# Plain and seven-product quads in turn, wider low parts and an eighth seven-product quad in eleven chunk pairs of a hybrid decoder layer

## The chip, the core and the metric

The kernel runs on one core of one Trainium2 chip. The time is that of one execution on the device in microseconds (us); the median of three runs is given, and one more execution was taken by the hardware profiler. Engines are named TensorE (PE in the profile, PEld its weight loads), VectorE (DVE), ScalarE (ACT), GpSimd (POOL) and SyncE (SP, which issues the loads here).

## What is computed

One layer works on 256 tokens of width 4096, in float32. One projection of 4096 x 16384 makes the inputs of an attention group (q, k, v and a gate z, 16 heads of 128) and of a short convolution group (h, B, C and a gate z). Both are gated, put side by side and mapped by an output projection of 4096 x 4096; a residual and an RMSNorm follow. With 256 tokens the block-sparse attention is causal attention in one block, with a bias by distance. Cut to what matters:

```
u = rmsnorm(x, norm_gain)
q, k, v, z_a, hc, b, c, z_c = split(u @ w_in)            # 4096 x 16384
attn = causal_attention(q, k, v, rel_bias) * silu(z_a)
conv = b * short_conv(c * hc, conv_w) * silu(z_c)        # three taps
h = x + concat(attn, conv) @ w_out                       # 4096 x 4096
out = rmsnorm(h, final_gain)
```

## The kernel before

**Products.** The weights stream once from HBM and are the moving operand; the tokens are the stationary one. The 32 column chunks of 512 of the input projection are taken in 16 pairs (0 to 15, `PAIRS`), those of the output projection in four more (16 to 19). Each pair runs over 16 quads. A quad is a block product of 2 x 2 blocks: two token blocks of 128 by two blocks of 128 of the inner dimension, times those two inner blocks by two chunks of 512. A plain quad makes the eight block products. A quad in `SEVENS` makes seven, by Strassen's scheme in Winograd's form, from sums of weight blocks (made on VectorE) and sums of token blocks (made once). A plain quad feeds the accumulators 3, 8, 2 and 4; a seven-product quad feeds 1, 3, 2 and then 5, 7, 6, 4. Accumulator n is PSUM bank `p`n, and there are eight banks.

**One block product is three matmuls.** Each operand is split into a high part in the fast float32 format and a low part, the rest. `block` (L552 to L563) makes stationary high by high, stationary low by high and stationary high by low, each with 512 columns, on lines 561, 562 and 563. The weights are split as they come, in `split` (L475): ScalarE writes the high part (L506), VectorE subtracts it for the low part (L507). A unit is what is split and multiplied at once: a plain quad has two units of 1024 (four blocks each), a seven-product quad one of 1536 from the raw weights (three blocks) and two of 1024 from the sums (two each). High and low parts lie in rings of three slots (`RING`), and the split runs two units ahead of the products. The sums come from three VectorE additions (L488 to L490) into one buffer, raw weights from loads of 1 MB, two quads ahead (`load`, L443).

**Ends of a pair.** In every pair but 0, 1 and 16 the quads 0, 2, ... 12 have seven products and the odd ones and 14 eight, in the order 0 to 15. So after position 12 the accumulators 1, 5, 6 and 7 are complete. `early` (L333) reads them at once, in one ScalarE copy and four VectorE additions (L336 to L340), and their banks serve as scratch for side tasks during the last 24 blocks. `scaled` (L349) multiplies the four early values by the row scale on ScalarE. The other four accumulators are read at the pair's end (`two_done`, L354; for the output `out_end`, L422).

**Side tasks.** `tasks_of` gives a list: after so many blocks behind the last seven-product quad, run a task. In the odd pairs 1 to 7 these are `turn` (transposes of q and k, copied by ScalarE), `scores` (two matmuls, bias and maxima on VectorE, exponentials on ScalarE) and `probs` (transposes, copied by ScalarE) for four heads; in the pairs 2, 4, 6 and 8 `values` and `mixed`; in 10, 12, 14 and at the head of 16 `conv`. The token sums that a seven-product quad needs are made for some quads only in pair 1 and pair 16 (`RAISE`, `made_up`), and the output's token operands during pairs 15 and 16 (`M_AT`, `m_parts`).

A scheduling layer sets each engine's order from this program; it can differ from the listing's order where the layer found another instruction ready first.

## Time and profile before

| | |
|---|---|
| median of three runs | 1729.7 us (1729.67 to 1729.95) |
| the profiled execution | 1729.5 us |
| its span, first to last instruction | 1727.7 us |
| busy: TensorE, VectorE, ScalarE | 99%, 87%, 59% of the span |
| mean granted TensorE clock | 0.998 |
| moved by DMA | 370 MB, 214 GB/s over the span |

The profiled execution's own time is 1.8 us over its span. The busy share of an engine counts the time in which any of its instructions is recorded; on TensorE the records of successive matmuls overlap, so the share doesn't tell how fast they follow each other. The granted clock is 1.00 but at the very end: the higher of the two levels, 2.4 GHz.

### The profile page before, as it was taken

The numbers are of one execution on the slowest core, as the hardware profiler recorded it, in microseconds if no ns is written. First come the engines' busy times: TensorE is split into PE (matmuls) and PEld (weight loads), VectorE is DVE, ScalarE is ACT, GpSimd is POOL, SyncE is SP. The second block draws the span as 40 slices with busy tenths as digits, with TensorE's granted clock in tenths as the row PEclk, the third lists the DMA queues.
The fourth block names the chain that finished last, engine by engine and source line by source line (L and its number), as shares of the span: only waits on it lengthen the run. The fifth ranks groups of instructions, "written<-read, shape, count | busy, mean of one in ns | idle before, by whom it ended". The sixth has DMA issues, their size and how long they took to land.

```text
span 1727.7 us, 20841 instructions
## 1 busy us (share of the span) xinstructions
PE 1711.7 (99%) x7672; PEld 1406.9 (81%) x7672; DVE 1498.8 (87%) x1658; ACT 1026.1 (59%) x1135; POOL 0.7 (0%) x6
## 2 busy tenths in 40 slices
...
GB/s 321 299 248 211 188 202 207 203 183 210 202 203 187 213 193 214 182 196 218 198 212 203 204 217 198 198 206 220 196 218 208 265 277 266 207 212 207 195 215 175
DMA packets 66562, 370.29 MB, mean 214 GB/s; under 512 B 8955, under 2 KB 13852, under 8 KB 25756
## 3 DMA queue, kind: packets, MB, share of 16 engines
...
HBM read 359.76 MB, written 9.18 MB: 214 GB/s over the span
## 4 chain that ended last, share of the span: by engine, by line
PE 97%; DVE 1%; ACT 1%; issue 0%; DVEq 0%; ACTq 0%
PE p L563 32%; PE p L561 31%; PE p L562 31%; PE p L239 0%; PE p L246 0%; ACT hi L506 0%; DVE lo L507 0%; PE p L108 0%; PE p L263 0%; PE p L272 0%; PE p L274 0%; PE p L273 0%; PE p L247 0%; PE p L298 0%; PE p L320 0%
## 5 line engine op out<-in xcount | busy, mean ns | idle before, releaser
L561 PE MATMUL p<-hi,k 128*128 128x512 f32 x2406 | 944.8, 393 | 2.9 <-ACT hi L506 2.8
L562 PE MATMUL p<-hi,k 128*128 128x512 f32 x2406 | 937.0, 389 | 0.0
L563 PE MATMUL p<-lo,k 128*128 128x512 f32 x2406 | 928.9, 390 | 0.1
L507 DVE TENSOR_TENSOR lo<-raw,hi 128x1024 fp32r<-128x1024 f32 (+2 forms) x508 | 676.2, 1348 | 61.3 <-ACT hi L506 60.3
L506 ACT CAST hi<-raw 128x1024 fp32r<-128x1024 f32 (+2 forms) x508 | 583.0, 1156 | 244.1 <-PE p L562 202.3
L561 PEld LDWEIGHTS p<-hi,k 128*128 128x128 f32 x2406 | 451.9, 188 | 100.1 <-ACT hi L506 9.0
L563 PEld LDWEIGHTS p<-lo,k 128*128 128x128 f32 x2406 | 451.3, 188 | 99.2 <-DVE lo L507 3.8
L562 PEld LDWEIGHTS p<-hi,k 128*128 128x128 f32 x2406 | 452.0, 188 | 91.0 <-issue 0.6
L506 ACT CAST hi<-sum 128x1024 fp32r<-128x1024 f32 x260 | 273.9, 1054 | 402.1 <-PE p L562 251.8
L507 DVE TENSOR_TENSOR lo<-sum,hi 128x1024 fp32r<-128x1024 f32 x260 | 317.6, 1221 | 127.1 <-ACT hi L506 125.7
L488 DVE TENSOR_TENSOR sum<-raw 128x1024 f32<-128x1024 f32 x130 | 158.8, 1222 | 9.7 <-DMA raw<-in_w_dram 8.0
L490 DVE TENSOR_TENSOR sum<-sum,raw 128x512 f32<-128x512 f32 x130 | 89.1, 685 | 0.3
L489 DVE TENSOR_TENSOR sum<-sum,raw 128x512 f32<-128x512 f32 x130 | 89.1, 685 | 0.1
L349 ACT ACTIVATE e<-e,rT 128x512 f32<-128x512 f32 x56 | 38.2, 717 | 0.0
L127 ACT CAST k<-c 128x512 fp32r<-128x512 f32 (+3 forms) x35 | 19.6, 576 | 10.9 <-PE p L563 6.0
L128 DVE TENSOR_TENSOR k<-c,k 128x512 fp32r<-128x512 f32 (+3 forms) x35 | 21.7, 632 | 0.8 <-ACT k L127 0.8
L424 ACT ACTIVATE e<-hg 128x512 f32<-128x512 f32 x16 | 10.0, 627 | 11.3 <-DVE hg L422 11.0
L277 DVE SCALAR_TENSOR_TENSOR am<-p,st,z 128x128 f32<-128x128 f32 x32 | 9.7, 344 | 7.5 <-PE p L274 7.5
L124 DVE TENSOR_TENSOR c<-c 128x128 f32<-128x128 f32 x56 | 14.0, 285 | 2.0 <-ACT c L138 1.2
L324 DVE SCALAR_TENSOR_TENSOR y<-p,cw,y 128x255 f32<-128x255 f32 (+1 forms) x32 | 15.3, 477 | 0.3 <-ACT y L322 0.2
L153 DVE SCALAR_TENSOR_TENSOR k<-xr,g_sb,k 128x256 fp32r<-128x256 f32 x26 | 11.6, 479 | 4.5 <-ACT k L152 4.5
L254 ACT ACTIVATE lg<-lg,st 128x256 f32<-128x256 f32 (+1 forms) x32 | 14.3, 446 | 0.0
...
## 6 DMA issues: line engine op xcount, KB each, us to landing
raw<-in_w_dram SPq DMA_DIRECT2D x254, 1024.0 KB, 4.8
...
```

Of the source, the lines that this page charges most:

```text
L127: nc.scalar.copy(dst[:, :, 0], c)
L128: nc.vector.tensor_tensor(dst[:, :, 1], c, dst[:, :, 0].bitcast(F32), ALU.subtract)
L324: nc.vector.scalar_tensor_tensor(y[:, i:], ps[:, :S - i], cw[:, k, 2 - i:3 - i], y[:, i:], op0=ALU.mult, op1=ALU.add)
L349: nc.scalar.activation(e, e, AF.Copy, scale=r)
L488: nc.vector.tensor_tensor(t[:, :2], raw[:, 1:3], raw[:, :1].to_broadcast([P, 2, B]), ALU.add)
L489: nc.vector.tensor_tensor(t[:, 2], t[:, 0], raw[:, 2], ALU.add)
L490: nc.vector.tensor_tensor(t[:, 3], t[:, 2], raw[:, 3], ALU.add)
L506: nc.scalar.copy(hi[:, c], src[:, c])
L507: nc.vector.tensor_tensor(lo[:, c], src[:, c], hi[:, c].bitcast(F32), ALU.subtract)
L561: nc.tensor.matmul(acc[b_], a, h_, start=s0, stop=False)
L562: nc.tensor.matmul(acc[b_], b, h_, start=False, stop=False)
L563: nc.tensor.matmul(acc[b_], a, l_, start=False, stop=s1)
```

## The change

1. The order in a pair begins with a plain quad, and plain and seven-product quads take turns. A pattern per pair says which: `P` takes the next plain quad, `S` the next seven-product one.
2. In the pairs 2 to 8 (pattern `8`) and 9, 11, 13, 15 (pattern `n`) quad 14 has seven products as well. Its token operand holds eight blocks (`BOTH`), as other pairs use it plain, and its sums are made in pair 1.
3. In odd pairs the accumulators 1, 2, 3, ... lie on other banks (`SWAP`): 1 and 2, 3 and 5, 4 and 6, 7 and 8 change places.
4. A plain quad is one unit of 2048: two high parts of 1024, one low part of 2048. Slots of the rings hold 2048 (1536 before). Units of three blocks and more issue all matmuls on high parts ahead of those on low parts (`AHEAD_HI`).
5. Sums go to two buffers in turn in pairs 0 to 15.
6. The side tasks stand within 16 blocks (two plain quads) behind the last seven-product quad, the last two `probs` of a group at the head of the next pair (`heads_of`); in patterns `n` no task stands there but the scalings, which go into the last plain quad. The scratch that the loader of the program reserves is set to 1024.

```diff
+PATS = {"7": "PSPSPSPSPSPSPSPP", "8": "PSPSSPSPSSPSPSPP", "n": "PSPSPSPSSPSPSPSP", "e": "PSPSPSPSPSPSSPPP"}
+KIND = "01888888" "8n7n7n7n" "077e"
 RING = 3
+SLOT = 4
+LO = 4
+HI = 2
+TS = (5, 7, 9, 11)
+AHEAD_HI = 8
...
-SEVEN = frozenset((0, 2, 4, 6, 8, 10, 12))
+SEVEN = tuple(range(0, 16, 2))
+EIGHT = tuple(range(1, 16, 2))
...
+SWAP = {1: 2, 2: 1, 3: 5, 5: 3, 4: 6, 6: 4, 7: 8, 8: 7}
...
+def of(pattern):
+    n = pattern.count("S")
+    return in_order(pattern, SEVEN[:n], EIGHT + SEVEN[n:]), set(SEVEN[:n])
...
-RAISE = {(1, 1): 4, (1, 3): 6, (1, 12): 0, (1, 14): 2,
+RAISE = {(1, 1): 4, (1, 3): 6, (1, 12): 0, (1, 13): 2, (1, 15): 14,
...
     def bank(n):
-        return ps_.tile([P, 512], F32, name=f"p{n}")
+        return ps_.tile([P, 512], F32, name=f"p{SWAP[n] if cur['p'] % 2 else n}")
...
-        return [(n, "raw", 0, (((1, 3), (0, 8)), ((1, 2), (0, 4)))),
-                (n, "raw", 2, (((3, 3), (2, 8)), ((3, 2), (2, 4))))]
+        a, b = (((1, 3), (0, 8)), ((1, 2), (0, 4))), (((3, 3), (2, 8)), ((3, 2), (2, 4)))
+        if n < LEAD or p == N_PAIRS + NDP - 1 and i >= KEPT:
+            return [(n, "raw", 0, a), (n, "raw", 2, b)]
+        return [(n, "raw", 0, a + b)]
...
-                t = sums[n] = wp.tile([P, 4, B], F32, name="sum")
+                k = sum(x in SEVENS[p] for x in ORDERS[p][:i])
+                t = sums[n] = (cur["pool"] if k % 2 and p < N_PAIRS else wp).tile([P, 4, B], F32, name="sum")
...
-            hi = wp.tile([P, 3 * B], F32R, name="hi", bufs=RING)
-            lo = wp.tile([P, 3 * B], F32R, name="lo", bufs=RING)
-        step = B if n < LEAD else m
+            hi = wp.tile([P, SLOT * B], F32R, name="hi", bufs=RING)
+            lo = wp.tile([P, SLOT * B], F32R, name="lo", bufs=RING)
+        step = B if n < LEAD else m if m < 4 * B else LO * B
         for a in range(0, m, step):
+            half = step if step < 2 * HI * B else HI * B
+            for b in range(a, a + step, half):
+                nc.scalar.copy(hi[:, b:b + half], src[:, b:b + half])
             c = slice(a, a + step)
-            nc.scalar.copy(hi[:, c], src[:, c])
             nc.vector.tensor_tensor(lo[:, c], src[:, c], hi[:, c].bitcast(F32), ALU.subtract)
...
+            for at, f, j, n in ((4, turn, 0, 1), (5, turn, 1, 6), (6, scores, 0, 7), (8, scores, 1, 5),
+                                (9, turn, 2, 1), (11, probs, 0, 6), (12, turn, 3, 7), (13, scores, 2, 5),
+                                (14, probs, 1, 1), (15, scores, 3, 6)):
+                put(at, f, p // 2 * HG + j, n)
...
-                put(4 + 5 * j, conv, (p - 10) // 2 * 4 + j, (1, 6, 7, 5)[j])
+                put(4 + 3 * j, conv, (p - 10) // 2 * 4 + j, (7, 5, 1, 6)[j])
...
+    def heads_of(p):
+        if p <= 8 and p % 2 == 0 and p:
+            return {6: [(probs, (p // 2 * HG - 2, 1))], 7: [(probs, (p // 2 * HG - 1, 6))]}
...
+        g = AHEAD_HI if len(products) > 2 and not late else 1
+        for j0 in range(0, len(todo), g):
+            for x in todo[j0:j0 + g] if g > 1 else ():
+                block(u, hi, lo, *x, what="h")
+            for x in todo[j0:j0 + g]:
+                block(u, hi, lo, *x, what="l" if g > 1 else "hl")
...
-                    tasks.setdefault(5 + 3 * j, []).append((scaled, (es[name], rows[c][:, t:t + 1])))
+                    tasks.setdefault(TS[j] if i < NQ - 2 else 4 + j, []).append((scaled, (es[name], rows[c][:, t:t + 1])))
```

The change moves instructions on every engine; three places are shown. A name's number is that of the buffer's use, `p` with a digit is a bank, `k` a quad's token operand. The changed program has other line numbers: L607, L608 and L610 are the three matmuls (L561 to L563 before), L542 the low part (L507), L521 to L523 the sums (L488 to L490), L353 and L355 the convolution's steps (L324, L326), L368 and L369 two of the early additions.

TensorE, from the last block of pair 16 into pair 17, before (`hi` and `lo` from the sums are those of bank p5):

```order
L561 MATMUL p4_10974<-hi_11612,k15_11412 128x512
L562 MATMUL p4_10974<-hi_11612,k15_11412 128x512
L563 MATMUL p4_10974<-lo_11613,k15_11412 128x512
L561 MATMUL p1_11687<-hi_11634,k0_10691 128x512
L562 MATMUL p1_11687<-hi_11634,k0_10691 128x512
L563 MATMUL p1_11687<-lo_11635,k0_10691 128x512
L561 MATMUL p5_11705<-hi_11650,k0_10691 128x512
L562 MATMUL p5_11705<-hi_11650,k0_10691 128x512
L563 MATMUL p5_11705<-lo_11651,k0_10691 128x512
L561 MATMUL p7_11709<-hi_11650,k0_10691 128x512
```

The same place now:

```order
L610 MATMUL p2_10630<-lo_11199,k15_11049 128x512
L610 MATMUL p4_10633<-lo_11199,k15_11049 128x512
L607 MATMUL p7_11311<-hi_11224,k1_10125 128x512
L608 MATMUL p7_11311<-hi_11224,k1_10125 128x512
L607 MATMUL p1_11314<-hi_11224,k1_10125 128x512
L608 MATMUL p1_11314<-hi_11224,k1_10125 128x512
L607 MATMUL p5_11308<-hi_11224,k1_10125 128x512
L608 MATMUL p5_11308<-hi_11224,k1_10125 128x512
L607 MATMUL p6_11317<-hi_11224,k1_10125 128x512
L608 MATMUL p6_11317<-hi_11224,k1_10125 128x512
L607 MATMUL p5_11308<-hi_11224,k1_10125 128x512
```

Before, the first products of pair 17 are those of a seven-product quad, and its second unit is made from a sum; now a plain quad's high parts come first, on banks p7, p1, p5 and p6.

VectorE at the end of pair 10 before, from the first convolution task (`y` is the convolution's result, `mt` its gated one, `p` with its digit the scratch bank that is read):

```order
L324 SCALAR_TENSOR_TENSOR y_7640<-p1_7635,cw_71,y_7640 128x255
L507 TENSOR_TENSOR lo_7647<-raw_7535,hi_7646 128x1024
L324 SCALAR_TENSOR_TENSOR y_7640<-p1_7635,cw_71,y_7640 128x254
L488 TENSOR_TENSOR sum_7724<-raw_7617 128x1024
L326 TENSOR_TENSOR mt_7644<-p1_7635,y_7640 128x256
L507 TENSOR_TENSOR lo_7667<-raw_7586,hi_7666 128x1024
L324 SCALAR_TENSOR_TENSOR y_7678<-p6_7673,cw_71,y_7678 128x255
L489 TENSOR_TENSOR sum_7724<-sum_7724,raw_7617 128x512
L324 SCALAR_TENSOR_TENSOR y_7678<-p6_7673,cw_71,y_7678 128x254
L507 TENSOR_TENSOR lo_7695<-raw_7586,hi_7694 128x1024
L326 TENSOR_TENSOR mt_7644<-p6_7673,y_7678 128x256
L324 SCALAR_TENSOR_TENSOR y_7709<-p7_7704,cw_71,y_7709 128x255
```

The same place now, from the third early value:

```order
L368 TENSOR_TENSOR e1_7421<-p5_6978,e1_7421 128x512
L369 TENSOR_TENSOR e3_7423<-p5_6978,e2_7422 128x512
L353 SCALAR_TENSOR_TENSOR y_7461<-p7_7456,cw_71,y_7461 128x255
L522 TENSOR_TENSOR sum_7486<-sum_7486,raw_7407 128x512
L353 SCALAR_TENSOR_TENSOR y_7461<-p7_7456,cw_71,y_7461 128x254
L523 TENSOR_TENSOR sum_7486<-sum_7486,raw_7407 128x512
L355 TENSOR_TENSOR mt_7465<-p7_7456,y_7461 128x256
L353 SCALAR_TENSOR_TENSOR y_7476<-p5_7471,cw_71,y_7476 128x255
L542 TENSOR_TENSOR lo_7491<-raw_7407,hi_7490 128x1536
L353 SCALAR_TENSOR_TENSOR y_7476<-p5_7471,cw_71,y_7476 128x254
L353 SCALAR_TENSOR_TENSOR y_7518<-p1_7513,cw_71,y_7518 128x255
L355 TENSOR_TENSOR mt_7465<-p5_7471,y_7476 128x256
```

Before, three low parts and two additions for the next sums lie between the steps of the first two tasks; now two additions and one low part lie between those that read p7 and p5, and the third task's first step comes ahead of the second's last.

VectorE in pair 17 before, a plain quad and a seven-product quad in steady turn:

```order
L507 TENSOR_TENSOR lo_11780<-raw_11699,hi_11779 128x1024
L507 TENSOR_TENSOR lo_11790<-raw_11699,hi_11789 128x1024
L488 TENSOR_TENSOR sum_11801<-raw_11725 128x1024
L507 TENSOR_TENSOR lo_11806<-raw_11725,hi_11805 128x1536
L489 TENSOR_TENSOR sum_11801<-sum_11801,raw_11725 128x512
L507 TENSOR_TENSOR lo_11822<-sum_11801,hi_11821 128x1024
L490 TENSOR_TENSOR sum_11801<-sum_11801,raw_11725 128x512
L507 TENSOR_TENSOR lo_11838<-sum_11801,hi_11837 128x1024
```

And in pair 4 now, where the pattern has two seven-product quads in a row (sums 3701 and 3759):

```order
L521 TENSOR_TENSOR sum_3701<-raw_3574 128x1024
L522 TENSOR_TENSOR sum_3701<-sum_3701,raw_3574 128x512
L542 TENSOR_TENSOR lo_3671<-sum_3576,hi_3670 128x1024
L523 TENSOR_TENSOR sum_3701<-sum_3701,raw_3574 128x512
L521 TENSOR_TENSOR sum_3759<-raw_3684 128x1024
L522 TENSOR_TENSOR sum_3759<-sum_3759,raw_3684 128x512
L542 TENSOR_TENSOR lo_3687<-raw_3515,hi_3686 128x2048
L542 TENSOR_TENSOR lo_3706<-raw_3574,hi_3705 128x1536
L542 TENSOR_TENSOR lo_3717<-sum_3701,hi_3716 128x1024
L523 TENSOR_TENSOR sum_3759<-sum_3759,raw_3684 128x512
L542 TENSOR_TENSOR lo_3745<-sum_3701,hi_3744 128x1024
```

Before, a plain quad has two low parts, and one sum buffer is filled after the other was read; now it has one low part of 2048, and the sum of the second seven-product quad is made ahead of the low parts of the first.

## Rows read from the trace of the kernel before

**Rows 1.** Page, part 1: busy us (share of the span) xinstructions.

```profile
PE 1711.7 (99%) x7672; PEld 1406.9 (81%) x7672; DVE 1498.8 (87%) x1658; ACT 1026.1 (59%) x1135; POOL 0.7 (0%) x6
```

**Rows 2.** Page, part 4: the chain that ended last, by line.

```profile
PE p L563 32%; PE p L561 31%; PE p L562 31%; PE p L239 0%; PE p L246 0%; ACT hi L506 0%; DVE lo L507 0%; PE p L108 0%; PE p L263 0%; PE p L272 0%; PE p L274 0%; PE p L273 0%; PE p L247 0%; PE p L298 0%; PE p L320 0%
```

**Rows 3.** Waits, whole run: waiter <- releaser: us in total, times, longest.

```profile
PEld p L561 <- ACT hi L506: 9.0, 20, 1.7
...
PEld p L563 <- DVE lo L507: 3.8, 12, 0.5
```

**Rows 4.** Timeline of TensorE, pair 11: start us, us, engine, line, what.

```profile
1000.17 0.39 PE L561 MATMUL p<-hi,k 128*128 128x512 f32 x1
...
1011.73 0.39 PE L561 MATMUL p<-hi,k 128*128 128x512 f32 x1
```

**Rows 5.** Lines by form: count | busy us, mean ns | idle before.

```profile
L561 PE MATMUL p<-hi,k 128*128 128x512 f32 x2406 | 944.8, 393 | 2.9 <-ACT hi L506 2.8
```

**Rows 6.** Timeline of VectorE, pair 11.

```profile
1007.67 1.22 DVE L507 TENSOR_TENSOR lo<-raw,hi 128x1024 fp32r<-128x1024 f32 x1
1008.81 0.68 DVE L489 TENSOR_TENSOR sum<-sum,raw 128x512 f32<-128x512 f32 x1
1009.41 1.75 DVE L507 TENSOR_TENSOR lo<-raw,hi 128x1536 fp32r<-128x1536 f32 x1
1011.08 0.68 DVE L490 TENSOR_TENSOR sum<-sum,raw 128x512 f32<-128x512 f32 x1
```

**Rows 7.** Stretches: length, PE, PEld, DVE, ACT, POOL busy, clock, DMA, GB/s.

```profile
1464.60:1482.00 17.40, 15.86 (x66) 11.45 (x64) 16.09 (x19) 11.46 (x18) 0.00 (x0) 1.00 0.49 166
877.00:894.40 17.40, 17.40 (x78) 14.27 (x77) 16.21 (x17) 11.08 (x10) 0.00 (x0) 1.00 0.46 172
...
270.80:359.10 88.30, 88.30 (x408) 73.17 (x407) 75.80 (x85) 55.62 (x70) 0.00 (x0) 1.00 0.52 182
961.20:1043.70 82.50, 82.50 (x365) 67.94 (x364) 72.31 (x72) 46.15 (x44) 0.00 (x0) 1.00 0.57 205
1294.60:1378.40 83.80, 83.69 (x373) 68.66 (x371) 79.86 (x90) 54.91 (x58) 0.00 (x0) 1.00 0.66 236
```

**Rows 8.** Waits between 1462 and 1484 us.

```profile
ACT hi L506 <- DVE sum L490: 5.9, 2, 3.0
```

**Rows 9.** Lines by form: splits, side tasks and end work.

```profile
L506 ACT CAST hi<-raw 128x1024 fp32r<-128x1024 f32 x370 | 386.8, 1052 | 189.8 <-PE p L562 165.7 <-ACT e L336 7.1 <-ACT e L349 4.0
...
L349 ACT ACTIVATE e<-e,rT 128x512 f32<-128x512 f32 x56 | 38.2, 717 | 0.0
...
L249 DVE TENSOR_TENSOR lg<-p,bt 128x384 f32<-128x384 f32 x16 | 8.8, 549 | 1.7 <-DMA bt<-bias_d 1.0 <-PE p L263 0.7
...
L254 ACT ACTIVATE lg<-lg,st 128x256 f32<-128x256 f32 x16 | 8.1, 505 | 0.0
...
L324 DVE SCALAR_TENSOR_TENSOR y<-p,cw,y 128x255 f32<-128x255 f32 x16 | 7.6, 478 | 0.2 <-ACT y L322 0.2
...
L326 DVE TENSOR_TENSOR mt<-p,y 128x256 f32<-128x256 f32 x16 | 6.7, 418 | 0.1
L253 DVE TENSOR_REDUCE st<-lg 128x1 f32<-128x256 f32 x16 | 6.7, 416 | 0.3
...
L354 DVE SCALAR_TENSOR_TENSOR k<-p,rT,e 128x512 f32<-128x512 f32 x8 | 6.0, 744 | 0.8 <-PE p L563 0.8
...
L254 ACT ACT_TABLE_LOAD x4 | 5.1, 1283 | 0.1
...
L253 DVE TENSOR_REDUCE st<-lg 128x1 f32<-128x128 f32 x16 | 4.4, 274 | 0.0
```

**Rows 10.** Timeline of TensorE, a convolution task in pair 10.

```profile
957.34 0.38 PE L318 MATMUL p<-ident,s 128*128 128x128 f32 x2
957.56 0.38 PE L320 MATMUL p<-ident,b 128*128 128x128 f32 x2
957.70 0.48 PE L561 MATMUL p<-hi,k 128*128 128x512 f32 x1
958.02 0.39 PE L562 MATMUL p<-hi,k 128*128 128x512 f32 x1
```

More of the change, by code (lines that the diff above doesn't have):

```diff
@@ L56, with in_order @@
 PAIRS += [x for g in range(4) for x in (((4, 6), g), ((7, 5), g))]
-ORDERS = [FIRST] + [USUAL] * (N_PAIRS - 1) + [FIRST] + [USUAL] * (NDP - 1)
-SEVENS = [SEVEN] * (N_PAIRS + NDP)
-SEVENS[0] = SEVENS[N_PAIRS] = SEVEN - {0, 2, 4, 6}
-SEVENS[1] = SEVEN - {0, 2}
-RAISE = {(1, 1): 4, (1, 3): 6, (1, 12): 0, (1, 14): 2,
+def in_order(pattern, seven, eight):
+    a, b = iter(seven), iter(eight)
+    return tuple(next(a) if x == "S" else next(b) for x in pattern)
+BOTH = SEVEN[-1]
+SIZES = [8 if q == BOTH else 7 if q in SEVEN else 4 for q in range(NQ)]
+def of(pattern):
+    n = pattern.count("S")
+    return in_order(pattern, SEVEN[:n], EIGHT + SEVEN[n:]), set(SEVEN[:n])
+ORDERS, SEVENS = zip(*([(FIRST, {8, 10, 12}), (USUAL, {4, 6, 8, 10, 12})]
+                       + [of(PATS[k]) for k in KIND[2:N_PAIRS]]
+                       + [(FIRST, {8, 10, 12})] + [of(PATS[k]) for k in KIND[N_PAIRS + 1:]]))
+RAISE = {(1, 1): 4, (1, 3): 6, (1, 12): 0, (1, 13): 2, (1, 15): 14,
          (N_PAIRS, 6): 0, (N_PAIRS, 8): 2, (N_PAIRS, 10): 4, (N_PAIRS, 12): 6}
@@ L116, in operands @@
     def operands(q):
-        A[q] = kt.tile([P, 7 if q in SEVEN else 4, 2, P], F32R, name=f"k{q}")
+        A[q] = kt.tile([P, SIZES[q], 2, P], F32R, name=f"k{q}")
         return A[q]
@@ L171, in made_up @@
         parts(A[q][:, 4:7], c[:, 4:7])
-        parts(A[q][:, :1], c[:, :1])
+        g = 7 if q == BOTH else 0
+        parts(A[q][:, g:g + 1], c[:, :1])
     def squares(n):
@@ L465, in units_of @@
     def units_of(n):
-        p, _, q = quads[n]
+        p, i, q = quads[n]
         if q in SEVENS[p]:
             return [(n, "raw", 1, (((1, 1),), ((6, 3),), ((3, 2),))),
-                    (n, "sum", 0, (((4, 5),), ((0, 7),))),
+                    (n, "sum", 0, (((4, 5),), ((7 if q == BOTH else 0, 7),))),
                     (n, "sum", 2, (((5, 6),), ((2, 4),)))]
-        return [(n, "raw", 0, (((1, 3), (0, 8)), ((1, 2), (0, 4)))),
-                (n, "raw", 2, (((3, 3), (2, 8)), ((3, 2), (2, 4))))]
+        a, b = (((1, 3), (0, 8)), ((1, 2), (0, 4))), (((3, 3), (2, 8)), ((3, 2), (2, 4)))
+        if n < LEAD or p == N_PAIRS + NDP - 1 and i >= KEPT:
+            return [(n, "raw", 0, a), (n, "raw", 2, b)]
+        return [(n, "raw", 0, a + b)]
     units = [u for n in range(len(quads)) for u in units_of(n)]
@@ L531, in tasks_of @@
             for j in range(4):
-                put(4 + 5 * j, conv, (p - 10) // 2 * 4 + j, (1, 6, 7, 5)[j])
+                put(4 + 3 * j, conv, (p - 10) // 2 * 4 + j, (7, 5, 1, 6)[j])
         return t
+    def heads_of(p):
+        if p <= 8 and p % 2 == 0 and p:
+            return {6: [(probs, (p // 2 * HG - 2, 1))], 7: [(probs, (p // 2 * HG - 1, 6))]}
+        if p == N_PAIRS:
+            t = {6 + 5 * j: [(conv, (12 + j, (1, 6, 7, 5)[j]))] for j in range(4)}
+            t[23] = [(open_out, ())]
+            return t
+        return {}
     ENDERS = ([x for g in range(4) for x in ((qk_end, g), (vz_end, g))]
@@ L552, in hymba_layer, with block @@
     last_of = {pb: x[-1] for pb, x in plan.items()}
-    def block(u, hi, lo, b0, a_, b_):
+    def block(u, hi, lo, b0, a_, b_, what="hl"):
         p, i, q = quads[units[u][0]]
@@ L557, in block @@
         s0, s1 = first_of[p, b_] == (u, a_), last_of[p, b_] == (u, a_)
-        if s0:
+        if s0 and "h" in what:
             acc[b_] = bank(b_)
         a, b = A[q][:, a_, 0], A[q][:, a_, 1]
-        nc.tensor.matmul(acc[b_], a, h_, start=s0, stop=False)
-        nc.tensor.matmul(acc[b_], b, h_, start=False, stop=False)
-        nc.tensor.matmul(acc[b_], a, l_, start=False, stop=s1)
+        if "h" in what:
+            nc.tensor.matmul(acc[b_], a, h_, start=s0, stop=False)
+            nc.tensor.matmul(acc[b_], b, h_, start=False, stop=False)
+        if "l" in what:
+            nc.tensor.matmul(acc[b_], a, l_, start=False, stop=s1)
     behind, tasks, kept, raised = None, {}, [], {}
@@ L572, in hymba_layer @@
         if start_of_quad and i == 0:
-            behind, tasks = None, {}
-            if p == N_PAIRS:
-                behind = 0
-                tasks = {5 + 5 * j: [(conv, (12 + j, (1, 6, 7, 5)[j]))] for j in range(4)}
-                tasks[22] = [(open_out, ())]
-            elif p > N_PAIRS:
+            behind, tasks = 0, heads_of(p)
+            if p > N_PAIRS:
                 out_load(p - N_PAIRS)
```

27 lines of the change are left out of this document (11 added, 16 removed).

## The prediction

> **What bounds the kernel now.** I read the page first: TensorE is busy for 1711.7 of 1727.7 us, VectorE for 1498.8 and ScalarE for 1026.1 [rows 1]. A busy TensorE may still be a waiting one, so the chain of waits comes next: the three matmul lines hold 32, 31 and 31% of the chain that ended last [rows 2]. The table of waits then says how little TensorE loses: its weight loads waited 9.0 us for high parts and 3.8 us for low parts in the whole run [rows 3]. So the time is the number of matmuls times the spacing of two of them. In the middle of a chunk pair 51 matmuls start in 1011.73 - 1000.17 = 11.56 us, that is 0.2267 us each [rows 4]; their recorded length of 393 ns overlaps the next one and is no price. There are 2406 blocks of three matmuls in the main group [rows 5] and 24 in the three late quads (eight each, by the code), 7290 matmuls in all, so 7290 x 0.2267 = 1653 us are the products themselves.
>
> VectorE is what the change loads. Its records overlap too: behind a low part of 1024 the next instruction starts after 1.14 us, though 1.22 are recorded; 512 wide it is 0.60 (recorded 0.68), 1536 wide 1.67 (recorded 1.75) [rows 6]. Each start comes 0.08 us before the recorded end of the one ahead. These spacings are the prices used below. For a low part of 2048 no row exists; 0.53 us for each further 512 gives 2.20 us, an estimate from these rows.
>
> **The change, part by part.**
>
> *Eleven more seven-product quads.* In pairs 2 to 9, 11, 13 and 15 an eighth quad takes seven blocks instead of eight: 2430 becomes 2419 blocks, 33 matmuls fewer. At 0.2267 us they are worth 7.5 us, all on the path that sets the end. The Trainium skill, page TensorE: Matmul & The Clock Gate, section Back-to-back issue gap, gives N/2.4 + 2.5 ns for a warm matmul, 216 ns at 512 columns; by it the 33 would be worth 7.1 us. The spacing in the trace is longer than that figure, and the sum goes by the trace.
>
> *Price of an eighth seven-quad on VectorE.* Sums 1.14 + 0.60 + 0.60 = 2.34 us, low parts 1.67 + 2 x 1.14 = 3.95, together 6.29, in place of 2 x 1.14 = 2.28 for a plain quad: 4.0 us more, 44 us in all. Joining two low parts of 1024 into one of 2048 saves 0.08 in 174 quads, 14 us. Net about 30 us on VectorE, 1499 to 1529, under 90% of the span. In steady alternation a plain and a seven-quad take 15 x 0.68 = 10.2 us on TensorE and 8.5 us on VectorE, so the cover holds. Two sevens in a row cost 12.6 us of VectorE against 9.5 of TensorE; the second sum buffer lets the sums of the second be made under the plain quad ahead, so its low parts alone (3.95) fall in its time. The tightest pair is 15, where VectorE is busy 79.9 of 83.8 us [rows 7] and gets 3.4 more (4.0 less eight times 0.08). It has 7.6 us more than pair 11 (72.3 of 82.5), the parts of the output operands, and its end (early values 4 x 0.60, end sums and their product, some 6 us) runs into pair 16 with nine plain quads at its head, each leaving 5.4 - 2.2 = 3.2 us free. I take 0 there, with bounds 0 to 3.
>
> *Plain quads first, banks in turn.* Now a pair starts with a plain quad whose banks were scratch or early banks of the pair before, and nothing waits for the end sums. Where this pays is seen at the start of pair 17: between 1464.6 and 1482.0 us TensorE issued 66 matmuls, in an equal stretch at the start of pair 10 it issued 78 [rows 7]. Twelve matmuls at 0.2267 are 2.7 us; the waits there name high parts on ScalarE that waited for a sum, 5.9 us in two waits [rows 8]. With a plain quad first, no sum is needed for 5.4 us. I take 2.4 us of gain, bounds 0 and 2.7. The other waits of [rows 3] I leave where they are; the third rival is their bound.
>
> *The ends of chunk pairs.* This is the open cost. Before, side work was spread over 24 blocks, one task every two or three; now there are two plain quads and the next pair's first plain quad, 16.3 us, and on VectorE everything meets there. I count in VectorE's order until a bank that the next plain quad needs is read. The low part of the first plain quad starts at -1.3 us from that quad's start: its slot's high part is read 3.4 us ahead, and two casts of 1.05 [rows 9] follow.
>
> Convolution ends (pairs 10, 12, 14), until bank p5 is free: three low parts 6.60, the early four 4 x 0.60, the next sums 2.34, a low part 1.67, five y steps of 0.478 - 0.08 and two products of 0.418 - 0.08 [rows 9], together 15.7, so 14.4 us after the start. TensorE comes there after 48 matmuls (10.9), four tasks of 0.36 + 0.09 [rows 10] and six matmuls on p7 (1.4): 14.1. So 0.3 us are lost, 0.9 in three pairs.
>
> Attention ends (pairs 1, 3, 5, 7), until bank p3 is free: 6.60 + 2.40 + 2.34 + 1.67, three bias adds of 0.549 - 0.08, two pairs of maxima (0.416 and 0.274, less 0.08 each: 0.53 a pair), two short reciprocals and three end sums of 0.744 - 0.08 [rows 9], 17.6 in all, so at 16.3. TensorE comes at 10.9 + 0.9 and ten of the twelve tasks, which cost a pair 88.3 - 82.5 = 5.8 us [rows 7], so 4.8: 16.6. Margin 0.3, cost 0. ScalarE's own chain there ends about as late: VectorE frees the last early value at 8.9, two scalings of 0.72, a table load of 1.28 and an exponential of 0.50 with a shorter one of half the columns behind it [rows 9] make some 12.5, and TensorE reaches the first transposes of probabilities after 44 matmuls (10.0) and five tasks of 5.8/12 us (2.4), at 12.4. That is 0.1 short, which I leave at 0. Pair 1 also raises quad 14 at its end, an estimated 1.5 us on each of the two engines by the lengths of like widths in [rows 9]: I take 0.5, bounds 0 and 1.5.
>
> At the eight-product ends (9, 11, 13, 15) only one plain quad stands behind the last seven. Until the second low part of the next seven: 4.40 + 2.40 + 2.34 + 1.67 + 4 x 0.66 + 1.14 = 14.6, at 13.3; TensorE needs it at 14.0. Cost 0. Even attention ends have less on VectorE: 0.
>
> The lower bound of all these ends is 0, as they hardly wait now. For the upper bound take every instruction at its recorded length, 0.08 more: 18, 22 and 14 instructions, so 1.8, 1.4 and 0.4 us are lost a time, 3 x 1.8 + 4 x 1.4 + 4 x 0.4 = 12.6 us, and about 3.5 more where the delay reaches the next seven-quad's last low part, 16 us. I take the spacings, as rows of the same engine under load show them.
>
> *Nothing else moves the end.* The scratch size only makes room; the load queue carries the same 318 loads of 1 MB; the tail keeps three late plain quads.
>
> **Sum.** The profiled execution took 1729.5 us, 0.2 under the median of the runs. 1729.5 - 7.5 - 2.4 + 0.9 + 0.5 = 1721.0, against the median 1721.2. I say **1721 us**.
>
> **Rivals.**
>
> *VectorE pays full lengths (slower).* At the chunk ends the queue of some 20 instructions may run at recorded lengths, since many wait for the one before. Then 16 us come back: 1729.7 - 7.5 - 2.4 + 16 + 0.5 = 1736. It decides, with the gain used up, once each start at an end lies some 0.05 us beyond the spacings of [rows 6]. For it: the ends hold dependent steps, and margins are 0.3 us. Against it: no start in [rows 6] is that late, and VectorE is idle for 13% of the span. The Trainium skill, page VectorE: DVE Perf Modes, section The DRAIN you can't avoid, says that the next op does not start until the pipe is empty, which would be this rival; in [rows 6] the next starts 0.08 us ahead of the recorded end, so the trace does not bear it out in mid-chunk. Chance 0.09.
>
> *Attention ends wait for ScalarE (no change).* ScalarE is in order, and a high part (1.5 us) and a table load stand between the transposes and the exponentials. If the exponentials are 2 us late in each of the four pairs, 8 us are lost and the gain is gone: 1721 + 8 = 1729. For it: the working above leaves no margin. Against it: the scheduler has set part of the tasks later than their listed places, under 16 matmuls that wait for no low part. Chance 0.17.
>
> *More waits go (faster still).* If nearly all 12.8 us of waits of weight loads [rows 3] were lost time and half went, 1729.7 - 7.5 - 6 = 1716. Chance 0.08.
>
> **How the numbers follow.** The forecast, 1717 to 1725, has 0.66. What a measurement can tell from no change is 0.2%, 3.5 us: faster means under 1726.2, slower over 1733.2. Faster gets the forecast and the third rival, 0.74; within 0.2% most of the second, 0.16; slower the first and what lies beyond it, 0.10. The range, 1716 to 1729, takes in the second rival and leaves the first out.
>
> **What would show it.** 2419 blocks with the spacing still near 0.227; a stretch behind the start of pair 17 as full as that of pair 10; VectorE at 1520 to 1540 us; waits of weight loads for low parts still below some 5 us. Low parts or bank reads as the releaser of matmuls at the ends of pairs 10, 12 and 14 would speak for the first rival, waits for ScalarE's lg or pt at the ends of 1, 3, 5 and 7 for the second. A gain under 4 us or over 14 would make this wrong.

## The result, and the profile after

The changed kernel takes **1720.1 us** (median of 4 runs, 1719.9 to 1720.4) against 1729.7 for the kernel before; the ratio is 0.9944 with a 95% interval of 0.9932 to 0.9956. The forecast was 1721.0, so 8.7 us less than the median; measured are 9.6. The profiled execution has a span of 1718.1 us (1727.7 before).

The page of the changed kernel, part 1 (busy us, share of the span, instructions) and part 4 (the chain that ended last, by engine), as [rows 1, 2]:

```profile
PE 1701.9 (99%) x7639; PEld 1402.2 (82%) x7639; DVE 1532.2 (89%) x1534; ACT 1014.3 (59%) x1152; POOL 0.7 (0%) x6
...
PE 94%; DVE 4%; issue 1%; ACT 0%; DVEq 0%; ACTq 0%
```

TensorE has 33 instructions fewer, VectorE is busy for 1532 us (forecast 1529). The chain is still that of the matmuls, but VectorE now holds 4% of it (1% before). The lines by form show the one low part of 2048, in 174 quads, at 2.29 us:

```profile
L542 DVE TENSOR_TENSOR lo<-raw,hi 128x2048 fp32r<-128x2048 f32 x174 | 396.2, 2286 | 53.7 <-PE p L610 37.0 <-ACT hi L540 16.2
```

The waits (waiter, releaser, us in total, times, longest), as [rows 3]:

```profile
PEld p L607 <- ACT hi L540: 3.6, 8, 0.9
...
PEld p L610 <- DVE lo L542: 1.5, 5, 0.4
...
PE p L607 <- DVE mt L355: 1.1, 3, 0.4
```

Waits for high parts fell from 9.0 to 3.6 us, those for low parts from 3.8 to 1.5. New are three waits for `mt`, the last reader of a convolution's scratch bank. The stretch behind the start of pair 17, beside an equal one in pair 10 (columns as in [rows 7]), is nearly full now, with 76 matmuls where 66 were:

```profile
1455.30:1472.70 17.40, 17.37 (x76) 13.92 (x75) 17.07 (x20) 9.44 (x15) 0.00 (x0) 1.00 0.46 152
868.70:886.10 17.40, 17.40 (x78) 14.39 (x77) 17.40 (x19) 11.20 (x12) 0.00 (x0) 1.00 0.43 169
```

Where the 9.6 us come from is seen by cutting both timelines of TensorE at each pair's first matmul (found by counting the matmuls of the three main lines: three for each block of a pair):

| pairs | before, us | after, us | difference | forecast |
|---|---|---|---|---|
| 0 | 88.10 | 86.39 | -1.71 | 0 |
| 1 | 90.06 | 89.00 | -1.06 | +0.5 |
| 2 to 9 | 692.45 | 687.03 | -5.42 | -5.4 |
| 10 to 14 | 417.60 | 417.33 | -0.27 | -0.8 |
| 15 and 16 | 169.98 | 169.28 | -0.70 | -0.4 |
| 17 | 85.27 | 83.03 | -2.24 | -2.4 |
| 18 | 82.87 | 82.93 | +0.06 | 0 |
| 19 with the tail | 94.96 | 96.82 | +1.86 | 0 |

(The start, up to the first matmul, is 0.11 shorter.) Some work crossed these cuts. Counted in the two traces, six of the 44 small TensorE instructions of pair 1 (the `probs` that change 6 put at the head of the next pair) stand in pair 2 now, six of each of the pairs 3, 5 and 7 in the pair behind, and eight of the convolution's went from pair 15 to 16. So pair 1 is to be read together with the pairs 2 to 9, and 15 with 16. Two things stand out: pairs 0 and 1 gained what the forecast had left out, and the tail lost more than half as much. The timeline of VectorE in the tail of the changed kernel (start us, duration):

```profile
1704.25 2.21 DVE L466 TENSOR_SCALAR hg<-hg,rf 128x512 f32<-128x512 f32 x4
1706.37 0.68 DVE L451 TENSOR_TENSOR hg<-p,hg 128x512 f32<-128x512 f32 x1
```

and of the kernel before:

```profile
1711.42 2.21 DVE L437 TENSOR_SCALAR hg<-hg,rf 128x512 f32<-128x512 f32 x4
...
1715.91 0.69 DVE L422 TENSOR_TENSOR hg<-p,hg 128x512 f32<-128x512 f32 x1
```

TensorE's last matmul starts at 1704.52 now and started at 1715.48 before. The last accumulator's addition followed it by 0.43 us; now it follows by 1.86, behind four scalings of the output's first half. In both kernels the end comes 11.7 to 11.8 us behind that addition. So 1.4 us of the loss in the table's last row lie behind the last matmul; the other 0.5 lie in the stream of pair 19 ahead of it (83.23 us up to the last matmul, 82.73 before).

### The profile page after: what moved, and what is told of

The parts are those of the page before. It is cut to its first block, busy times and chain, and to the rows that moved or that the text cites. A ratio compares the mean times of both kernels' runs of the same rounds, so it can differ in the third digit from the quotient of the medians.

```text
span 1718.1 us, 20350 instructions
## 1 busy us (share of the span) xinstructions
PE 1701.9 (99%) x7639; PEld 1402.2 (82%) x7639; DVE 1532.2 (89%) x1534; ACT 1014.3 (59%) x1152; POOL 0.7 (0%) x6
## 4 chain that ended last, share of the span: by engine, by line
PE 94%; DVE 4%; issue 1%; ACT 0%; DVEq 0%; ACTq 0%
PE p L607 31%; PE p L608 31%; PE p L610 30%; DVE lo L542 1%; PE p L275 0%; DVE hg L454 0%; PE p L268 0%; DVE y L353 0%; DVE sum L521 0%; PE p L292 0%; PE p L136 0%; ACT hi L540 0%; DVE hg L466 0%; PE p L303 0%; PE p L302 0%
## 5 line engine op out<-in xcount | busy, mean ns | idle before, releaser
L607 PE MATMUL p<-hi,k 128*128 128x512 f32 x2395 | 933.6, 391 | 1.8 <-DVE mt L355 1.1
L608 PE MATMUL p<-hi,k 128*128 128x512 f32 x2395 | 932.5, 390 | 0.0
L542 DVE TENSOR_TENSOR lo<-raw,hi 128x2048 fp32r<-128x2048 f32 (+2 forms) x323 | 644.1, 2013 | 66.3 <-PE p L610 37.0
L610 PE MATMUL p<-lo,k 128*128 128x512 f32 x2395 | 701.1, 392 | 0.0
L540 ACT CAST hi<-raw 128x1024 fp32r<-128x1024 f32 (+2 forms) x497 | 550.7, 1165 | 236.5 <-PE p L608 197.9
L607 PEld LDWEIGHTS p<-hi,k 128*128 128x128 f32 x2395 | 449.5, 188 | 99.8 <-ACT hi L540 3.6
L608 PEld LDWEIGHTS p<-hi,k 128*128 128x128 f32 x2395 | 449.6, 188 | 92.9 <-issue 0.6
L610 PEld LDWEIGHTS p<-lo,k 128*128 128x128 f32 x2395 | 446.8, 188 | 91.2 <-DVE lo L542 1.5
L540 ACT CAST hi<-sum 128x1024 fp32r<-128x1024 f32 x282 | 296.3, 1051 | 370.6 <-PE p L608 263.5
L542 DVE TENSOR_TENSOR lo<-sum,hi 128x1024 fp32r<-128x1024 f32 x282 | 342.6, 1221 | 82.8 <-PE p L610 74.3
L521 DVE TENSOR_TENSOR sum<-raw 128x1024 f32<-128x1024 f32 x141 | 171.9, 1219 | 4.5 <-DMA raw<-in_w_dram 3.9
L522 DVE TENSOR_TENSOR sum<-sum,raw 128x512 f32<-128x512 f32 x141 | 97.1, 688 | 2.5
L523 DVE TENSOR_TENSOR sum<-sum,raw 128x512 f32<-128x512 f32 x141 | 96.9, 687 | 1.8
L353 DVE SCALAR_TENSOR_TENSOR y<-p,cw,y 128x255 f32<-128x255 f32 (+1 forms) x32 | 14.7, 475 | 1.0 <-ACT y L351 1.0
L454 DVE TENSOR_TENSOR hg<-hg,c 128x512 f32<-128x512 f32 x16 | 10.7, 689 | 2.8 <-ACT e L453 2.8
```

The costliest lines, as they stand in the source:

```text
L521: nc.vector.tensor_tensor(t[:, :2], raw[:, 1:3], raw[:, :1].to_broadcast([P, 2, B]), ALU.add)
L522: nc.vector.tensor_tensor(t[:, 2], t[:, 0], raw[:, 2], ALU.add)
L523: nc.vector.tensor_tensor(t[:, 3], t[:, 2], raw[:, 3], ALU.add)
L540: nc.scalar.copy(hi[:, b:b + half], src[:, b:b + half])
L542: nc.vector.tensor_tensor(lo[:, c], src[:, c], hi[:, c].bitcast(F32), ALU.subtract)
L607: nc.tensor.matmul(acc[b_], a, h_, start=s0, stop=False)
```

## The experiments

Line numbers in rows of an experiment can be some lines higher than in the changed kernel. Differences are to the changed kernel where nothing else is said.

### The eleven sevens taken back

```diff
-KIND = "01888888" "8n7n7n7n" "077e"
+KIND = "01777777" "77777777" "077e"
```

> Every pair with an eighth seven-product quad goes back to seven of them (11 quads take eight products again: 33 more matmuls); order, banks and buffers stay. My theory (TensorE's number of matmuls sets the time, VectorE has cover): 33 x 0.2267 = 7.5 us more than the changed kernel, 1727.6, between 1726.5 and 1728.5. Rival (VectorE's 44 us of extra work for the sevens is partly paid on the path): VectorE gets them back, so clearly less than 7.5 is lost, 1724 or below. Second rival (order and banks earn the gain, not the products): 1722 or below.

Measured: 1727.2 us, ratio to the kernel before 0.9986 (0.9977 to 0.9995). Each of the eleven pairs is longer by 0.64 to 0.74 us, most by 0.68, which is 3 x 0.2267. VectorE's busy time fell to 1492.7 us, 40 less, and gave nothing back. So the rival that VectorE's work is paid on the path falls, and the products earn what their number says. The Trainium skill (TensorE: Matmul & The Clock Gate, Back-to-back issue gap) gives 216 ns as the gap of a single matmul by itself and 131 ns for a stream of weight loads and matmuls; by these it would be 0.65 or 0.39 a pair. The trace's spacing of 226.7 is above both, and it is the one that the time follows.

### The old order with the new sevens

```diff
-PATS = {"7": "PSPSPSPSPSPSPSPP", "8": "PSPSSPSPSSPSPSPP", "n": "PSPSPSPSSPSPSPSP", ...
+PATS = {"7": "SPSPSPSPSPSPSPPP", "8": "SPSSPSPSPSPSPSPP", "n": "SPSSPSPSPSPSPSPP", ...
...
-        return ps_.tile([P, 512], F32, name=f"p{SWAP[n] if cur['p'] % 2 else n}")
+        return ps_.tile([P, 512], F32, name=f"p{n}")
```

> Each pair starts with a seven-product quad again, and the banks do not change places; the eleven eighth sevens, the low parts of 2048 and the second sum buffer stay. My theory: what plain-first and the banks earn is what was seen at pair starts, 2.2 us at pair 17, 1.4 in pair 0 and some 1 to 2 at pairs 15 and 16, so 3 to 6 us more: 1723 to 1726. Rival (order and banks earn most of the gain): 1728 or more. Second rival (they earn nothing, the sevens do all): 1719 to 1721.

Measured: 1727.1 us, 0.9985 (0.9976 to 0.9993): 7.0 us more, just over my range and under the rival's. Pair 2 is 2.9 us longer, pair 17 2.8, pair 4 1.6. In pairs 2 and 17 TensorE waits for high and low parts, and the high parts had waited for sums (6.0 and 9.9 us there); in pair 4 it waits for VectorE's read of a bank in the scores (`lg`, 1.3 us). The waits of weight loads in the whole run:

```profile
PEld p L607 <- ACT hi L540: 8.6, 16, 1.5
...
PEld p L610 <- DVE lo L542: 5.1, 10, 0.8
```

Taking back the sevens costs 7.1 us, taking back the order 7.0, and both stand in a change that is worth 9.6. So either the two need each other, or the rest of the change costs some 4.5 us by itself; the kernel with neither was not run. For the first speak pairs 2 and 4: in the old order without the eighth seven they took 86.2 us each before, with it 88.7 and 87.5. There it costs time instead of saving 0.68, even if six small instructions that came from the pair ahead, some 0.8 us by the 6.0 us that 44 of them cost pair 3, are taken off. For the second speak the length of the low parts and the tail below, 3.3 and 1.9 us. Some of the tail comes back here: the four scalings start 3.40 us before TensorE's last matmul, and the end comes 12.59 us behind that matmul's start, where it is 13.59 in the changed kernel and 12.23 in the kernel before. The places of the side tasks (change 6) were taken back in no run.

### The banks not swapped

```diff
-        return ps_.tile([P, 512], F32, name=f"p{SWAP[n] if cur['p'] % 2 else n}")
+        return ps_.tile([P, 512], F32, name=f"p{n}")
```

> Plain quads still come first in a pair, but the banks no longer change places between odd and even pairs, so that a pair's first plain quad writes the very banks that the end sums of the pair before still read. My theory: at each of 18 pair starts TensorE waits for end sums that stand behind VectorE's queue of a pair's end, at least the 1 us of one end sum and its start, up to the some 4 us by which two plain quads fall short: 20 to 70 us more, 1740 to 1790. Rival (the banks do not matter since the scheduler finds other matmuls): within 2 us of the changed kernel, 1718 to 1722.

Measured: 1752.7 us, 1.0133 (1.0119 to 1.0147), 32.7 more, within the range; but the loss is not at each of 18 starts. Pairs 2 to 9 are within 0.2 us of the changed kernel; pairs 10, 12, 14 and 15 are each 5 to 6 us longer, 17 3.5, 18 2.0, 19 1.8, 11 and 13 1.4. The waits that TensorE itself shows name low parts more than the readers of banks:

```profile
PE p L610 <- DVE lo L542: 10.6, 6, 2.0
PE p L607 <- DVE mt L355: 3.9, 3, 1.3
```

And not all of it is waiting. At the starts of pairs 10, 12, 14, 16 and 17, each time in or right behind a wait of TensorE of 1.5 to 2.0 us, the granted clock fell to 0.5, the lower of the two levels (1.2 GHz), for 20.5 us in all. One of these stretches, at the start of pair 12 (columns as in [rows 7]):

```profile
1049.26:1052.67 3.41, 3.41 (x10) 2.67 (x9) 3.41 (x5) 2.10 (x2) 0.00 (x0) 0.50 0.70 288
```

Matmuls follow each other at 0.427 us there and not at 0.227; 44 of them at 0.2 more are some 9 of the 32.7 us, an estimate from the trace of this run. In this kernel a plain quad first is a loss without banks that are free.

### Low parts of 1024

```diff
-LO = 4
+LO = 2
```

> Low parts of 1024 in place of 2048 in the plain quads: about 0.08 us more of VectorE in each of some 170 quads, 14 us in all. My theory: hidden in mid-chunk; at the three convolution ends, where VectorE ends last, three or four such pieces cost 0.24 to 0.32 us each: 0 to 1 us more, 1720 to 1721. Rival (VectorE pays everywhere): 5 to 14 us more, 1725 to 1734.

Measured: **1716.7 us**, 0.9924 (0.9911 to 0.9936), 3.3 less. Both theories had it slower: a miss. The page shows VectorE at 1537.3 us, only 5 more. TensorE no longer waits for `mt`. The timeline of VectorE at the end of pair 10 shows what changed; the changed kernel first:

```profile
943.38 0.68 DVE L366 TENSOR_TENSOR e<-p,e 128x512 f32<-128x512 f32 x1
943.98 2.28 DVE L542 TENSOR_TENSOR lo<-raw,hi 128x2048 fp32r<-128x2048 f32 x1
946.18 0.68 DVE L367 TENSOR_TENSOR e<-p,e 128x512 f32<-128x512 f32 x1
...
950.49 0.68 DVE L523 TENSOR_TENSOR sum<-sum,raw 128x512 f32<-128x512 f32 x1
951.09 0.42 DVE L355 TENSOR_TENSOR mt<-p,y 128x256 f32<-128x256 f32 x1
...
951.82 1.75 DVE L542 TENSOR_TENSOR lo<-raw,hi 128x1536 fp32r<-128x1536 f32 x1
...
954.27 0.41 DVE L355 TENSOR_TENSOR mt<-p,y 128x256 f32<-128x256 f32 x1
```

and TensorE, which waits for that second `mt` (bank p5):

```profile
953.82 0.63 PE L610 MATMUL p<-lo,k 128*128 128x512 f32 x2
954.83 0.47 PE L607 MATMUL p<-hi,k 128*128 128x512 f32 x1 [0.38 <-DVE mt L355]
```

With low parts of 1024, whose pair 10 ends 1.6 us later on its clock:

```profile
944.15 0.68 DVE L366 TENSOR_TENSOR e<-p,e 128x512 f32<-128x512 f32 x1
...
951.44 0.41 DVE L355 TENSOR_TENSOR mt<-p,y 128x256 f32<-128x256 f32 x1
...
952.76 0.42 DVE L355 TENSOR_TENSOR mt<-p,y 128x256 f32<-128x256 f32 x1
953.10 0.68 DVE L523 TENSOR_TENSOR sum<-sum,raw 128x512 f32<-128x512 f32 x1
953.70 1.75 DVE L542 TENSOR_TENSOR lo<-raw,hi 128x1536 fp32r<-128x1536 f32 x1
```

The second `mt` comes 1.5 us earlier although pair 11 starts 1.6 us later (954.45 against 952.89): three us of margin. Of these, 0.8 lie ahead of the first early value (L366): it starts 10.3 us before pair 11 here, 9.5 in the changed kernel. The rest is order: the changed kernel has the third addition for the sums, the low part of 1536 and one step of the convolution ahead of the second `mt`, and here they stand behind it. With the shorter pieces the scheduling layer put what frees a bank further forward; no run kept the order and changed the pieces alone.

### 1024 at the pair ends alone

```diff
-        step = B if n < LEAD else m if m < 4 * B else LO * B
+        end = i == 0 or not any(x in SEVENS[p] for x in ORDERS[p][i:])
+        step = B if n < LEAD else m if m < 4 * B else (2 if end else 4) * B
```

> Low parts of 1024 only in a pair's first plain quad and in the plain quads behind its last seven-product quad; 2048 elsewhere. After the run with 1024 everywhere (1716.7 us, 3.3 less than the changed kernel) two theories stand. Theory of grain: a low part of 2048 holds VectorE for 2.2 us, and at a pair's end the instructions that free banks stand behind it; then the ends alone matter, and this kernel gives most of the 3.3 us back: 1716.5 to 1717.5. Rival (grain counts in mid-chunk too, or the gain there came from a lucky order of the matmuls): 1718.5 to 1720.5.

Measured: 1716.5 us, 0.9925 (0.9913 to 0.9938). Pieces of 1024 at the ends give all of it: pairs 11, 13 and 15 go from 82.3 to 81.62 us, 17 and 18 from 83.0 to 82.3. 120 blocks at 3 x 0.2267 are 81.6, so nothing is left in those three. So the pieces in mid-chunk do not count, within the noise. The rival's lucky order is not ruled out as a cause: VectorE's order at the end of pair 10 has the low part of 1536 behind the second `mt` here too. What speaks against luck is that the next run, with yet another order, has the same 81.62 us in those three pairs.

### Low parts of 512

```diff
-LO = 4
+LO = 1
```

> Low parts of 512 everywhere in plain quads: four pieces for one, 0.24 us more of VectorE in each of some 174 quads than in the changed kernel, 42 us, VectorE at about 1574 us. Theory of grain (a piece of 1024 is already fine enough, mid-chunk has cover): the ends gain no more than with 1024 and the load is hidden except in pair 15, where VectorE is at 97%: 1716.5 to 1719. Rival (VectorE is so near its limit that load beyond the 1024 kernel is paid): 1722 or more.

Measured: 1718.2 us, 0.9932 (0.9918 to 0.9945), as the theory of grain said. VectorE is busy for 1554.6 us: 522 more instructions cost 22 us, 0.04 each and not the 0.08 of the prediction. Against the kernel with 1024 at the ends, pair 18 is 0.75 us longer and pair 1 0.34; pair 15, where the theory had put the loss, is the same.

### VectorE's load at the convolution ends

```diff
-        nc.vector.tensor_tensor(w_, acc[5], u, ALU.subtract)
+        for _ in range(3 if cur["p"] in (10, 12, 14) else 1):
+            nc.vector.tensor_tensor(w_, acc[5], u, ALU.subtract)
```

> The changed kernel, with the last of the four early values computed three times at the ends of pairs 10, 12 and 14: two more VectorE instructions of 512 columns (0.60 us each) ahead of the bank that the next pair's first plain quad waits for. My theory (VectorE's order sets when that bank is free, TensorE waits there for 0.55 us now): each of them is paid in full, 3 x 1.2 = 3.6 us more than the changed kernel, 1723.7, between 1723 and 1724.5. Rival (the 0.55 us wait has another source and VectorE has slack there): 1720 to 1721.5.

Measured: 1723.7 us, 0.9964 (0.9951 to 0.9976), the forecast to 0.1. The first matmul on p5 waited longer (idle 1.58 us where 0.38 stood), and pairs 11, 13 and 15 are 1.2 us longer each:

```profile
956.79 0.47 PE L608 MATMUL p<-hi,k 128*128 128x512 f32 x1 [1.58 <-DVE mt L355]
```

Two instructions cost 1.21 to 1.24 us at each end, twice the spacing of 0.60 and not twice the recorded 0.68. That is the price that the prediction's first rival denied. The Trainium skill's sentence that the next op waits until the pipe is empty (VectorE: DVE Perf Modes, The DRAIN you can't avoid) does not make the recorded length the price here. The same section of the Trainium skill adds that a next op that is not held starts earlier, and the trace agrees: starts lie 0.08 us ahead of the recorded ends.

### One sum buffer

```diff
-                t = sums[n] = (cur["pool"] if k % 2 and p < N_PAIRS else wp).tile([P, 4, B], F32, name="sum")
+                t = sums[n] = wp.tile([P, 4, B], F32, name="sum")
```

> All sums of the chunk pairs share one buffer again. In 19 places two seven-product quads follow each other; there the sums of the second (2.34 us of VectorE) can only be made when the high and low parts of the first are done. My theory: VectorE then needs 12.6 us against 9.5 of TensorE in two such quads, and what lies ahead in the ring covers a part: 0.5 to 2 us lost each time, 10 to 40 in all, 1730 to 1758. Rival (the second buffer is idle insurance): 1719 to 1722.

Measured: 1722.2 us, 0.9957 (0.9942 to 0.9972): 2.1 more, just over the rival's range and far under the theory's. By the patterns it is 18 places; the nineteenth, in pair 19, had one buffer all along. The loss is in pairs 2 (0.75), 15 (0.48) and 4 (0.44); elsewhere it is under 0.1 us, and why is not shown.

### Block by block in plain quads

```diff
-AHEAD_HI = 8
+AHEAD_HI = 1
```

> In a plain quad the three matmuls of a block follow each other again, in place of 16 with high parts and then 8 with low parts; the low part is one of 2048 still. My theory: in steady state the low parts are made early enough, but at pair ends VectorE is some 15 us deep and the low part of the next pair's first plain quad is then needed 3.2 us earlier: 1 to 3 us lost at each of some 10 ends, 1730 to 1750. Rival (VectorE is ahead everywhere): 1719 to 1723.

Measured: 1756.2 us, 1.0153 (1.0139 to 1.0167), 36 more, 6 above my range. Weight loads waited 45.0 us for low parts (1.5 in the changed kernel), and not at ends alone: pair 0 is 3.8 us longer, the others 0.7 to 2.6.

```profile
PEld p L610 <- DVE lo L542: 45.0, 119, 1.7
```

With a low part of 2048, high parts first are worth these 36 us; what they are worth with low parts of 1024 was not run.

### Scalings moved out of the tail

```diff
-            if n == 2:
+            if n in on_pool:
+                nc.gpsimd.tensor_scalar(row, row, rf, None, op0=ALU.mult)
+            elif n == 2:
...
-    finish(0)
+    rf0 = finish(0)
+    rows_out(0, rf0, (0, 1, 2))
...
-    finish(1)
+    rows_out(0, rf0, (3, 4), (4,))
+    rows_out(1, finish(1))
```

> In the tail, of the five scalings of the first half of the output only two short ones stay on VectorE ahead of the last accumulator's sum; one of 1024 goes behind that sum and one of 1024 to GpSimd. My theory: the changed kernel loses about 1.4 us because the last sum waits on VectorE for four scalings (it starts at 1706.37, while TensorE's last matmul started at 1704.52 and 0.43 us is the distance seen before); with the two short ones ahead it starts at about 1704.95, so 1.4 us less: 1718.7, between 1718.2 and 1719.2. Rival (the end is set by the store of the first half or by something else): no change, 1720; slower if GpSimd takes over some 5 us for its 1024 columns.

Measured: 1720.3 us, 0.9943 (0.9929 to 0.9956): no change, the rival's value. The timeline of VectorE and GpSimd:

```profile
1704.64 0.48 DVE L473 TENSOR_SCALAR hg<-hg,rf 128x512 f32<-128x512 f32 x1
...
1705.05 1.34 DVE L473 TENSOR_SCALAR hg<-hg,rf 128x512 f32<-128x512 f32 x1
...
1706.91 1.48 DVE L473 TENSOR_SCALAR hg<-hg,rf 128x1024 f32<-128x1024 f32 x1
...
1711.28 0.75 DVE L473 TENSOR_SCALAR hg<-hg,rf 128x1024 f32<-128x1024 f32 x1
```

```profile
1704.78 3.06 POOL L469 TENSOR_SCALAR hg<-hg,rf 128x1024 f32<-128x1024 f32 x1 [1703.49 <-DVE rf L220]
```

GpSimd works from 1704.78 to 1707.84. A scaling of 512 on VectorE beside it took 1.34 us (0.48 alone), one of 1024 1.48 (0.75 alone). The addition came at 1706.31, 1.40 behind the last matmul instead of 1.86, and its product then waited for the slowed scaling. So the experiment does not decide what the tail is worth; a version that spares VectorE without GpSimd was not run. The Trainium skill (SBUF — State Buffer, SBUF: two separate sides) calls the port that the two share an exclusive lock, held for the whole instruction. The slowing agrees in kind; but the scaling that started at 1705.05 ended at 1706.39, 1.4 us ahead of GpSimd's, so "fully blocks" is more than the trace shows (with the care that the profile's spans on GpSimd are rough).

### An eighth seven in three more pairs, and in five

```diff
-KIND = "01888888" "8n7n7n7n" "077e"
+KIND = "01888888" "8n8n8n8n" "077e"
```

(on the kernel with 1024 at the ends)

> The kernel with low parts of 1024 at the pair ends alone (1716.5 us), with an eighth seven-product quad in pairs 10, 12 and 14 too: 9 matmuls fewer. My theory (TensorE's number of matmuls sets the time while VectorE has cover): 9 x 0.2267 = 2.0 us less, 1714.4, between 1713.8 and 1715. Rival (these pairs have the convolutions on VectorE, 76.4 of 84.2 us busy, and 4 us more each brings the waits at their ends back): 1715.5 to 1718.

Measured: **1714.3 us**, 0.9910 (0.9897 to 0.9924), the fastest of the case and 5.7 below the changed kernel. Pairs 10, 12 and 14 are 0.5 to 0.65 us shorter.

```diff
-KIND = "01888888" "8n8n8n8n" "077e"
+KIND = "01888888" "8n8n8n8n" "088e"
...
-         (N_PAIRS, 6): 0, (N_PAIRS, 8): 2, (N_PAIRS, 10): 4, (N_PAIRS, 12): 6}
+         (N_PAIRS, 6): 0, (N_PAIRS, 8): 2, (N_PAIRS, 10): 4, (N_PAIRS, 12): 6, (N_PAIRS, 15): 14}
```

> As the run before, and an eighth seven-product quad in pairs 17 and 18 (its operand raised in pair 16): 15 matmuls fewer than with low parts of 1024 at the ends alone. My theory: 15 x 0.2267 = 3.4 us less than 1716.5, 1713.1, between 1712.3 and 1714. Rival (pairs 17 and 18 share one sum buffer and hold the output sums, 75 of 83 us busy; raising one more operand in pair 16 loads VectorE and ScalarE there): the 1.4 us of these two pairs are not had, 1714.2 to 1716.

Measured: 1720.0 us, 0.9943 (0.9930 to 0.9955), 5.6 more than with three: on the rival's side, and far beyond it. Pair 17 is 3.3 us longer than with three, pair 18 1.9, though each has a product fewer. VectorE in pair 17, where two seven-product quads follow each other on one sum buffer:

```profile
1472.14 1.23 DVE L543 TENSOR_TENSOR lo<-sum,hi 128x1024 fp32r<-128x1024 f32 x1 [1.19 <-ACT hi L541]
1473.40 1.23 DVE L521 TENSOR_TENSOR sum<-raw 128x1024 f32<-128x1024 f32 x1
...
1477.95 0.68 DVE L523 TENSOR_TENSOR sum<-sum,raw 128x512 f32<-128x512 f32 x1
```

and ScalarE and TensorE behind it:

```profile
1478.74 1.04 ACT L541 CAST hi<-sum 128x1024 fp32r<-128x1024 f32 x1 [2.96 <-DVE sum L523]
```

```profile
1479.84 0.50 PE L608 MATMUL p<-hi,k 128*128 128x512 f32 x1 [1.02 <-ACT hi L541]
```

The second sum starts right behind the low part that reads the first, is done at 1478.63, and TensorE waits. That fits the lack of a second buffer in the output pairs; a run with one there was not made. It is not the single buffer alone: all waits of pair 17 lie 19.9 to 28.9 us behind its start, and the pair's second place with two sevens in a row has none. Why the same single buffer cost so little in pairs 5 to 8 of the run with one buffer stays open.

## Why the prediction was right, point by point

*Eleven sevens, -7.5.* Right: pairs 2 to 9 gave 5.42 of 5.44, and taken back they cost 0.68 each, 7.1 in all.

*VectorE's load is hidden.* Right in mid-chunk (1532 us for 1529). Joining the low parts was priced at 14 us of VectorE; it is 5 in the busy time. More important, the step asked only what the joined low part costs VectorE in sum, not what else moves when a piece of 2.2 us stands at a pair's end. That costs 3.3 us, and the cut into 1024 at the ends has them back. It was the largest thing that I did not see. How much of it is the length of the piece and how much the order that the scheduling layer makes around it is not shown; in the rows of pair 10 the order is the larger part.

*Plain first and the banks, -2.4.* Pair 17 gave 2.24. But taking the part back costs 7.0 us once the sevens are there, in pairs 2, 4 and 17 above all: the step priced it against the kernel before and not together with the other part.

*Convolution ends, +0.9.* Right in place and releaser, 0.55 us a time and not 0.3: 1.65. The excess sat where the count said, behind p5, and added load showed that the spacings are the prices there.

*Attention ends and pair 1, +0.5.* The ends cost nothing. Pairs 3, 5 and 7 gained 0.9 to 1.2, where the products alone are 0.68, but they handed small instructions on to the pairs behind, which gained only 0.3 to 0.6: two neighbours together gained 1.3 to 1.5 for a product count of 1.36. Pair 1 handed on six as well, so its 1.06 is read with the pairs 2 to 9: 6.48 us together, 1.0 more than the products. Together with pair 0 (-1.71, where a wait of TensorE for a high part, 1.4 us, is gone) this is part of the third rival. With high parts first pair 0 takes 86.4 to 86.8 us in every run, block by block 88.1 before and 90.2 with the low part of 2048; so the order of high parts, which I had given no price, seems to serve there.

*"Nothing else moves the end."* This step failed: the tail lost 1.86. The tail does keep three late plain quads, but the scheduling layer drew some of their matmuls ahead of the last ones on the first two accumulators: VectorE's first end sums start 6.2 us before TensorE's last matmul, where they started 8.4 before it. The first half's scalings start 0.27 us before TensorE's last matmul, where they started 4.06 before it, and no longer hide under it. With the old order they start 3.40 us before it again, and 1.0 us of the tail comes back.

*Sum.* Missed gains of 3.3 us (pairs 0 and 1) and missed losses of 2.6 (tail, convolution ends) nearly cancel, and pairs 15 and 16 gave 0.3 beyond forecast. That the forecast of 1721 is good to 0.9 us is partly luck for that reason; the 7.5 us for the products is not.

*Rivals.* Full lengths on VectorE: a sign that was named for it, reads of banks as releasers at the ends of pairs 10, 12 and 14, did show, but the load added at these ends rules it out: the price there is the spacing. ScalarE at the attention ends: no wait of TensorE for `lg` or `pt` in those pairs stands out, and their lengths fell. More waits go: half true, and given back in the tail.
